# Key norms of a hybrid RWKV-7 and FoX block: the sum of squares by products with a block of ones, the root on the channels

## The chip, the cores and the metric

The kernel runs on one core of one Trainium2 chip. A core has a matrix engine (TensorE, PE in the profile, with its weight loads as PEld), a vector engine (VectorE, DVE), a scalar engine with lookup tables for functions (ScalarE, ACT), GpSimd (POOL) and SyncE (SP), which here only issues loads. The metric is the time of one execution on the device in microseconds (us).

## The reference, cut to what matters

The input has 256 positions of 2048 channels; 16 learned positions are put in front, so the kernel works on L = 272 positions. One layer projects them, runs RWKV-7 time mixing (16 heads of 64 channels) and FoX forgetting attention (16 heads of 64) beside each other, merges the two under gates and ends with a feed-forward network. The change touches two norms over the 64 channels of a head, at each position:

```python
# RWKV-7: the key that removes from the state
kk = heads((k * k_k).astype(F32))
kk = kk / jnp.maximum(jnp.sqrt(jnp.sum(kk * kk, axis=-1, keepdims=True)), 1e-12)
...
# FoX: queries and keys
def _rms(x, g):
    xf = x.astype(F32)
    xf = xf * lax.rsqrt(jnp.mean(xf * xf, axis=-1, keepdims=True) + RMS_EPS)
    return xf.astype(x.dtype) * g
q = _rms(q.reshape(B, L, FOX_HEADS, HEAD_DIM), q_g)
k = _rms(k.reshape(B, L, FOX_HEADS, HEAD_DIM), k_g)
```

The input of the projections is itself normalised (`_rms(h, n1)`). The kernel leaves the factor 1/rms of each position (`rsb`) out of the weight products and brings it in behind them.

## The kernel before, in words

**Weight products.** Every number is float32. For the matrix engine a number is split in a high half, which is its value in the engine's short float32r form, and a low half, the rest; a product is then made of three (high by high, high by low, low by high). Weights come in blocks of 128x1024 (512 KB). `wload` makes one: SyncE issues the load into `raw`, ScalarE copies it to the high half `wh` (L350), VectorE subtracts to get the low half `wl` (L351). Each of `raw`, `wh` and `wl` has three buffers, so `wh` of block n+3 is written when TensorE is done with block n. The products of channels by positions are L361, L362, L363 (272 or 258 columns) and, where only the 256 real positions are wanted, L420 and L422, with high and low half of the activations side by side in 512 columns.

**Groups.** The heads are worked in four groups of four. For each group g the loop runs, on TensorE, the weight products of RWKV's k, v and r (256 columns of weights each), of the small low-rank maps (`sig`, `aa`, `g`), of FoX's q, k and v, and two jobs of output gates (`zg`); behind the four groups come the remaining gates, the branches, the output and the feed-forward network (`gt`, `up`, `dn`).

**Order of the work.** The work that doesn't use weights (norms, state updates, attention) is written as generators, which the code calls streams. A clock of estimated nanoseconds runs with the weight products: after each product group `slot(ns)` adds its estimate, and when a stream's due time has come, its next stage is emitted at this place, one stage at a slot. A stage ends in `yield delay`, which sets the next due time. TensorE's instructions stand in exactly the order in which the code emits them (`manual_schedule`); the other engines' instructions are ordered by a scheduler that models their durations, and each engine then runs them strictly in its order, waiting for the operands of the next one. Of the on-chip sums (PSUM), four banks hold weight products and four (`aux_ps`) are for the streams.

**RWKV's k norm** (`rwkv_bg`, one stream per group). ScalarE makes `kk` = k times `k_k` and its square `sq`. In `head_sums` six float32 products have a tile of squares (positions as rows) as weights and `bsum`, two columns of ones for the two heads of a tile, as moving data; the sums lie with positions on the partitions, 12 numbers each. The profile counts each float32 product twice (`ss`, L383). Nine small VectorE passes (`rsqrt_steps`, L239 to L248, in two stages) give the root's reciprocal from the bits of the number and two refinements. `spread` copies it on ScalarE to 64 channels per head; six float32 transposes on TensorE bring it back to channels by positions (`kx`, L387), and VectorE multiplies `k` by it from PSUM (L708). Then come the decay's scans and exponentials, the operands `ar` and `bk` (L735, L732), and the products `mat`. A later stage of the same stream, group by group, is the normalised output `Y` (L960), which TensorE transposes (`yT`, L387), 4200 ns (`NORM`) of the clock later.

**FoX's norms** (`fox_jobs`). The squares of q (`sqf`, two halves) go through `head_sums` (`fss`: four float32 products, eight rows), and so do the squares of k (six products, twelve rows). A stream `norms` waits for both, takes the root of all 20 numbers at once, and spreads k's part back as above (`fx`, six transposes, a multiplication of `kn`). q's root stays with positions on the partitions, where the attention uses it as a scale (`hs`, `hr`). The attention `fox_bg` waits for `ready`, loads its bias and goes on to the scores `sc`.

The state update of group g-1 (`u`, `y`, `s` and copies, in the `step` stages) runs beside the beginning of group g.

## Time and profile before

| | |
|---|---|
| three runs | 1586.58, 1588.59, 1588.29 us |
| median | 1588.29 us |
| the profiled execution | 1585.63 us, of it the span of the page 1583.9 us |
| granted TensorE clock | 1.0 |
| TensorE, products | busy 1573.6 us (99%), 10292 |
| TensorE, weight loads | busy 1371.4 us (87%) |
| VectorE | busy 1007.9 us (64%), 1849 |
| ScalarE | busy 771.5 us (49%), 1133 |
| GpSimd | busy 109.7 us (7%), 207 |

How to read the rows. A row of a timeline gives the start in us from the span's beginning, the length, the engine, the line of the kernel, the operation, output<-input by the program's names, sizes, and how many like instructions in a row it stands for (x); a bracket tells how long the engine had been idle before it and what ended that. Weight products overlap, so the distance of two starts, and not the length, is what a product takes of TensorE's time. A row of groups gives busy time and mean nanoseconds of one, then the idle time just before these instructions with what ended it. A row of stretches gives from:to, then PE with its busy time, the sum of its weight loads and products (with counts), VectorE, ScalarE and GpSimd busy in the stretch, the granted clock, the share of the DMA engines and GB/s.

### The profile page before, as it was taken

The numbers are of one execution on the slowest core, as the hardware profiler recorded it, in microseconds if no ns is written. First come the engines' busy times: TensorE is split into PE (matmuls) and PEld (weight loads), VectorE is DVE, ScalarE is ACT, GpSimd is POOL, SyncE is SP. The second block draws the span as 40 slices with busy tenths as digits, with TensorE's granted clock in tenths as the row PEclk, the third lists the DMA queues.
The fourth block names the chain that finished last, engine by engine and source line by source line (L and its number), as shares of the span: only waits on it lengthen the run. The fifth ranks groups of instructions, "written<-read, shape, count | busy, mean of one in ns | idle before, by whom it ended". The sixth has DMA issues, their size and how long they took to land.

```text
span 1583.9 us, 26384 instructions
## 1 busy us (share of the span) xinstructions
PE 1573.6 (99%) x10292; PEld 1371.4 (87%) x10292; DVE 1007.9 (64%) x1849; ACT 771.5 (49%) x1133; POOL 109.7 (7%) x207
## 2 busy tenths in 40 slices
PE   8999999999999999999999999999999999999998
PEld 7998988889889878999888888888888888888887
DVE  5777677768868856776556656655666566444443
ACT  6555455455445544654445544544455445333332
POOL 4103102203101200000000000000000000000000
PEclk9999999999999999999999999999999999999999
DMA  7655546545544556776756666666666666566664
GB/s 204 177 156 167 146 121 174 167 127 142 167 143 139 169 161 176 243 227 210 225 178 180 184 195 186 186 186 187 186 186 184 189 186 187 188 204 203 188 200 132
DMA packets 217132, 283.34 MB, mean 179 GB/s; under 512 B 26554, under 2 KB 134704, under 8 KB 217008
## 3 DMA queue, kind: packets, MB, share of 16 engines
q1 hardware_dynamic: 212144, 277.68, 59.6%
q10 hardware_dynamic: 4320, 3.93, 0.7%
q8 instruction: 81, 1.33, 0.3%
q14 instruction: 43, 0.35, 0.1%
q0 software_dynamic: 544, 0.05, 0.0%
HBM read 274.43 MB, written 7.19 MB: 178 GB/s over the span
## 4 chain that ended last, share of the span: by engine, by line
PE 99%; DVE 0%; DMA 0%; ACT 0%; SPq 0%; issue 0%; ACTq 0%
PE up L420 10%; PE gt L420 10%; PE zg L420 8%; PE dn L1255 5%; PE dn L1256 5%; PE dn L1254 5%; PE up L422 5%; PE gt L422 5%; PE zg L422 4%; PE f L361 2%; PE f L420 2%; PE f L363 2%; PE f L362 2%; PE br L362 2%; PE br L363 2%; PE br L361 2%
## 5 line engine op out<-in xcount | busy, mean ns | idle before, releaser
L351 DVE TENSOR_TENSOR wl<-raw,wh 128x1024 fp32r<-128x1024 f32 (+2 forms) x512 | 613.5, 1200 | 447.4 <-ACT wh L350 446.4
L350 ACT ACTIVATE wh<-raw 128x1024 fp32r<-128x1024 f32 (+2 forms) x512 | 530.1, 1038 | 613.3 <-PE dn L1255 142.4
L420 PE MATMUL gt<-hts,wh 128*128 128x512 f32 x704 | 247.0, 398 | 0.0
L420 PE MATMUL up<-hts,wh 128*128 128x512 f32 x704 | 247.0, 398 | 0.0
L422 PE MATMUL gt<-hts,wl 128*128 128x256 f32 x660 | 185.5, 281 | 0.0
L422 PE MATMUL up<-hts,wl 128*128 128x256 f32 x660 | 185.2, 281 | 0.0
L420 PE MATMUL zg<-xhl,wh 128*128 128x512 f32 x512 | 184.6, 404 | 0.0
L420 PEld LDWEIGHTS up<-hts,wh 128*128 128x128 f32 x704 | 130.1, 188 | 28.8
L420 PEld LDWEIGHTS gt<-hts,wh 128*128 128x128 f32 x704 | 129.9, 188 | 28.6
L1255 PE MATMUL dn<-wh,acl 128*128 128x512 f32 x352 | 138.9, 395 | 0.0
L1256 PE MATMUL dn<-wl,ach 128*128 128x512 f32 x352 | 138.9, 395 | 0.0
L1254 PE MATMUL dn<-wh,ach 128*128 128x512 f32 x352 | 138.9, 395 | 0.0
L422 PE MATMUL zg<-xhl,wl 128*128 128x256 f32 x480 | 135.0, 281 | 0.0
L422 PEld LDWEIGHTS up<-hts,wl 128*128 128x128 f32 x660 | 124.6, 189 | 1.9
L422 PEld LDWEIGHTS gt<-hts,wl 128*128 128x128 f32 x660 | 124.6, 189 | 1.9
L420 PEld LDWEIGHTS zg<-xhl,wh 128*128 128x128 f32 x512 | 94.4, 188 | 21.6 <-issue 1.8
L422 PEld LDWEIGHTS zg<-xhl,wl 128*128 128x128 f32 x480 | 90.6, 189 | 1.1
L1255 PEld LDWEIGHTS dn<-wh,acl 128*128 128x128 f32 x352 | 66.3, 188 | 15.6
L1254 PEld LDWEIGHTS dn<-wh,ach 128*128 128x128 f32 x352 | 66.3, 188 | 15.5
L1256 PEld LDWEIGHTS dn<-wl,ach 128*128 128x128 f32 x352 | 66.3, 188 | 15.4
L361 PE MATMUL f<-xhl,wh 128*128 128x272 f32 x256 | 77.6, 303 | 0.0
L363 PE MATMUL f<-xhl,wl 128*128 128x272 f32 x256 | 73.8, 288 | 0.0
(467 smaller groups left out, 2798.4 us busy)
## 6 DMA issues: line engine op xcount, KB each, us to landing
raw<-in_w_gate_up_dram SPq DMA_DIRECT2D x176, 512.0 KB, 3.7
raw<-in_w_in_dram SPq DMA_DIRECT2D x160, 512.0 KB, 3.8
raw<-in_w_down_dram SPq DMA_DIRECT2D x88, 512.0 KB, 3.8
raw<-in_w_o_dram SPq DMA_DIRECT2D x32, 512.0 KB, 4.3
raw<-in_w_branch_a_dram SPq DMA_DIRECT2D x16, 512.0 KB, 3.6
raw<-in_w_branch_b_dram SPq DMA_DIRECT2D x16, 512.0 KB, 4.7
zgd<-zg ACTq DMA_DIRECT2D x30, 128.0 KB, 1.8
gate<-zgd SPq DMA_DIRECT2D x15, 256.0 KB, 4.6
```

The lines of the kernel that those rows point to most:

```text
L350: nc.scalar.activation(wh[:prow, cs_], raw[:prow, cs_], AF.Copy)
L351: nc.vector.tensor_tensor(wl[:prow, cs_], raw[:prow, cs_], wh[:prow, cs_].bitcast(F32), op=ALU.subtract)
L361: nc.tensor.matmul(ps, wh, ah, start=first, stop=False)
L362: nc.tensor.matmul(ps, wh, al, start=False, stop=False)
L363: nc.tensor.matmul(ps, wl, ah, start=False, stop=last)
L420: nc.tensor.matmul(ps.rearrange("p (a t) -> p a t", a=2), wh, act, start=first, stop=last)
L422: nc.tensor.matmul(ps[:, :T], wl, act[:, 0, :], start=False, stop=False)
L1254: nc.tensor.matmul(box[t], ah[:, kt, ts_], wh[:, k, :], start=first, stop=False)
L1255: nc.tensor.matmul(box[t], al[:, kt, ts_], wh[:, k, :], start=False, stop=False)
L1256: nc.tensor.matmul(box[t], ah[:, kt, ts_], wl[:, k, :], start=False, stop=last)
```

## The change

Three things are done in another way.

First, for RWKV's k and FoX's k the sum over a head and its way back to the channels become one step. The squares (channels by positions, 128x272 for each half m of the group) are split in float32r high and low halves (`nh` on ScalarE, `nl` on VectorE), and each half is multiplied with `bones`, the 128x128 matrix with two blocks of 64x64 ones, which the kernel already has for another sum. The result has, on each channel, its head's sum. Per norm these are four float32r products of 272 columns, where there were 6 float32 products with 2 columns (12 rows) and 6 transposes.

Second, the root is taken on all channels: a floor or an added term comes out of PSUM on VectorE into the place of the squares (`floor`), ScalarE takes Ln and then Exp with scale -0.5, which is a first value of the root's reciprocal, and five VectorE passes over 128x272 per half (ten in all, L634 to L638 of the changed kernel) refine it and multiply `kk` or `kn`. In between stand two delays of the clock, `N_SUM` = 1200 and `N_ROOT` = 2000; `X_RS`, `X_SPREAD` and `Y_SPREAD` go.

Third, FoX's q keeps its way (`head_sums`, small passes, now over 8 numbers, in `q_norms`, a stream of its own), and k gets `k_norms`. The term added to k's mean square was `eps1`, with positions on the partitions; it is now `epsw`, over channels by positions, made once at the start by three VectorE operations, among them a reciprocal over 128x272. The Ln and Exp of FoX's norm write into a tile that shares its single buffer with the attention's bias. GpSimd's eight memsets for padded sums go.

```diff
+    epsw = xp.tile([P, L], F32, tag="epsw", name="epsw")
...
             nc.vector.tensor_copy(rsb, prb)
+
+            nc.vector.tensor_tensor(epsw, rsb, rsb, op=ALU.mult)
+            nc.vector.reciprocal(epsw, epsw)
+            nc.vector.tensor_scalar(epsw, epsw, RMS_EPS, None, op0=ALU.mult)
...
+    def head_norms(xs, root, dst, floor, name):
+        parts = []
+        for m in range(2):
+            hi, lo_ = (zt_(f"{n}{name}{m}")[:, :L].bitcast(F32R) for n in ("nh", "nl"))
+            split(hi, lo_, xs[m])
+            parts.append((hi, lo_))
+        yield N_SUM
+        pss = []
+        for m in range(2):
+            ps = aux_ps(f"{name}{m}")[:, :L]
+            for i, part in enumerate(parts[m]):
+                clock[2] += L / 2.4
+                nc.tensor.matmul(ps, bones, part, start=i == 0, stop=i == 1)
+            pss.append(ps)
+        for m in range(2):
+            floor(xs[m], pss[m])
+        ys = root()
+        for m in range(2):
+            nc.scalar.activation(ys[m], xs[m], AF.Ln)
+        for m in range(2):
+            nc.scalar.activation(ys[m], ys[m], AF.Exp, scale=-0.5)
+        yield N_ROOT
+        for m in range(2):
+            x_, y_ = xs[m], ys[m]
+            nc.vector.tensor_tensor(x_, x_, y_, op=ALU.mult)
+            nc.vector.tensor_tensor(x_, x_, y_, op=ALU.mult)
+            nc.vector.scalar_tensor_tensor(x_, x_, -10.0 / 3.0, x_, op0=ALU.add, op1=ALU.mult)
+            nc.vector.scalar_tensor_tensor(y_, x_, 5.0, y_, op0=ALU.add, op1=ALU.mult)
+            nc.vector.scalar_tensor_tensor(dst[:, m, :], y_, 0.375, dst[:, m, :], op0=ALU.mult, op1=ALU.mult)
...
-        for d, ps in head_sums(kn_, [sq[:, m, :] for m in range(2)], L, f"ss{g}"):
-            nc.vector.tensor_scalar(d, ps, 1e-24, None, op0=ALU.max)
-        yield from rsqrt_steps(rw, kr_, kn_, [P, 12], "kt")
-        backs = [spread(kr_, m, L, f"kx{g}{m}") for m in range(2)]
-        yield Y_SPREAD
-        for m in range(2):
-            nc.vector.tensor_tensor(kk[:, m, :], kk[:, m, :], backs[m](), op=ALU.mult)
+        def root():
+            y = et(f"ny{g}")
+            return [y[:, m, :] for m in range(2)]
+        yield from head_norms([sq[:, m, :] for m in range(2)], root, kk,
+                              lambda x_, ps: nc.vector.tensor_scalar(x_, ps, 1e-24, None, op0=ALU.max), f"ss{g}")
         yield Y_KK
...
+        def q_norms(sqs):
+            for i, (d, ps) in enumerate(head_sums(hs, sqs, f"fss{g}")):
+                nc.vector.tensor_scalar(d, ps, 1.0 / HD, eps1[:, i:i + 1], op0=ALU.mult, op1=ALU.add)
+            yield from rsqrt_steps(fx, hr, hs, [P, 8], "ht")
+
+            nc.vector.tensor_tensor(hs, hs, hr, op=ALU.mult)
+            ready.append(1)
+
+        def k_norms(sqs):
+            def root():
+                y = fx.tile([P, 2, L], F32, tag="bias", name=f"fy{g}", bufs=1)
+                return [y[:, m, :] for m in range(2)]
+            yield from head_norms(sqs, root, kn,
+                                  lambda x_, ps: nc.vector.scalar_tensor_tensor(
+                                      x_, ps, 1.0 / HD, epsw, op0=ALU.mult, op1=ALU.add), f"fk{g}")
             ready.append(1)
...
-                    spawn(sums(sqs, dst, n), SUMS)
-                    if dst is kn:
-                        spawn(norms(), PREP)
+                    spawn((q_norms if dst is qn else k_norms)(sqs), SUMS)
...
-        while not ready or not gate_done:
+        while len(ready) < 2 or not gate_done:
```

The scheduler orders the engines anew. The rows below are instructions in an engine's order: line, operation, output<-inputs, size and count. A name is the program's name with its group's digit and a number of its tile.

VectorE at RWKV's k norm of group 1, before: the floors (L703) and small passes of the root between low halves of weights (`wl`) and copies of the state (`sv`).

```order
L351 TENSOR_TENSOR wl_2798<-raw_2796,wh_2797 128x1024
L703 TENSOR_SCALAR kn1_2778<-ss1_2780 128x4 x2
L703 TENSOR_SCALAR kn1_2778<-ss1_2780 16x4
L239 TENSOR_SCALAR kr1_2779<-kn1_2778 128x12
L240 TENSOR_TENSOR kt_2791<-kr1_2779 128x12
L241 SCALAR_TENSOR_TENSOR kt_2791<-kn1_2778,kt_2791 128x12
L351 TENSOR_TENSOR wl_2844<-raw_2842,wh_2843 128x1024
L242 SCALAR_TENSOR_TENSOR kr1_2779<-kt_2791,kr1_2779 128x12
L244 TENSOR_TENSOR kt_2791<-kr1_2779 128x12
```

The same place after the change: floors (L718), ten passes with nothing between them, FoX's q halves (L431), and only then the next `wl`.

```order
L718 TENSOR_SCALAR sq1_2774<-ss10_2841 128x272
L718 TENSOR_SCALAR sq1_2774<-ss11_2844 128x272
L634 TENSOR_TENSOR sq1_2774<-sq1_2774,ny1_2849 128x272 x2
L635 TENSOR_TENSOR sq1_2774<-sq1_2774,ny1_2849 128x272 x2
L636 SCALAR_TENSOR_TENSOR sq1_2774<-sq1_2774 128x272 x2
L637 SCALAR_TENSOR_TENSOR ny1_2849<-sq1_2774,ny1_2849 128x272 x2
L638 SCALAR_TENSOR_TENSOR k1_2000<-ny1_2849,k1_2000 128x272 x2
L431 TENSOR_TENSOR qn1_2676<-qn1_2676,f01_0_2732 128x256
L431 TENSOR_TENSOR qn1_2676<-qn1_2676,f01_1_2733 128x256
L355 TENSOR_TENSOR wl_2909<-raw_2907,wh_2908 128x1024
```

The floor's result goes to ScalarE and comes back as `ny1` between the second and the third of these rows, so VectorE stands there until Exp is done.

VectorE around the scaled output `Y` in group 1, before: `Y` (L960), then FoX's root passes, the meta products' masks (L767), and one `wl` before the copies out of `yT` (L973).

```order
L960 TENSOR_TENSOR Y0_2506<-Y0_2506,s20_3063 128x512
L241 SCALAR_TENSOR_TENSOR ht_3209<-hs1_2647,ht_3209 128x20
L242 SCALAR_TENSOR_TENSOR hr1_2648<-ht_3209,hr1_2648 128x20
L244 TENSOR_TENSOR ht_3209<-hr1_2648 128x20
L245 SCALAR_TENSOR_TENSOR ht_3209<-hs1_2647,ht_3209 128x20
L246 SCALAR_TENSOR_TENSOR ht_3209<-ht_3209 128x20
L247 TENSOR_SCALAR ht_3209<-ht_3209 128x20
L767 TENSOR_TENSOR NK01_3095<-mat010_3223,mup_77 80x2x16
L767 TENSOR_TENSOR NK01_3095<-mat011_3224,mup_77 80x2x16
L248 TENSOR_TENSOR hr1_2648<-ht_3209,hr1_2648 128x20
L351 TENSOR_TENSOR wl_3303<-raw_3301,wh_3302 128x1024
L973 COPY ya_118<-yT0_3255 64x4x64 x2
```

After: FoX's low half of the squares (L492), the masks (L777) and a `wl` stand ahead of `Y` (L970).

```order
L492 TENSOR_TENSOR nlfk11_3176<-sqf11_3142,nhfk11_3175 128x272
L244 TENSOR_TENSOR gt_3065<-s20_3042 128x8
L777 TENSOR_TENSOR NK01_3074<-mat010_3194,mup_77 80x2x16
L245 SCALAR_TENSOR_TENSOR gt_3065<-s10_3041,gt_3065 128x8
L777 TENSOR_TENSOR NK01_3074<-mat011_3195,mup_77 80x2x16
L246 SCALAR_TENSOR_TENSOR gt_3065<-gt_3065 128x8
L355 TENSOR_TENSOR wl_3282<-raw_3280,wh_3281 128x1024
L247 TENSOR_SCALAR gt_3065<-gt_3065 128x8
L248 TENSOR_TENSOR s20_3042<-gt_3065,s20_3042 128x8
L970 TENSOR_TENSOR Y0_2459<-Y0_2459,s20_3042 128x512
L983 COPY ya_119<-yT0_3226 64x4x64 x2
```

On TensorE `yT` itself moves up: it stood in the third of the four blocks of FoX's v weights and now stands in the second, three products behind the last of `mat`; the block whose `wh` buffer `wh_3281` takes over is the first.

ScalarE at RWKV's k norm of group 0, after: between the two high halves of the squares (L491) stands a `wh` of weights, and the two table loads stand before Ln and before Exp.

```order
L712 ACTIVATE sq0_1174<-k0_591 128x544
L491 ACTIVATE nhss00_1191<-sq0_1174 128x272
L354 ACTIVATE wh_1235<-raw_1234 128x1024
L491 ACTIVATE nhss01_1195<-sq0_1174 128x272
L628 ACT_TABLE_LOAD
L628 ACTIVATE ny0_1221<-sq0_1174 128x272 x2
L630 ACT_TABLE_LOAD
L630 ACTIVATE ny0_1221<-ny0_1221 128x272 x2
L430 ACTIVATE qn0_1085<-f00_0_1141 128x256
```

Before, `sq0` was followed there by weight blocks and the copies of `spread`; there was no table load in the norm.

More of the change, by code (lines that the diff above doesn't have):

```diff
@@ L592, in forget_gate, with head_sums @@
         gate_done.append(1)
[L596 to L599 removed]
+    def head_sums(dst, sqs, name):
         ps = aux_ps(name)
[L603 to L605 removed]
+        for i in range(2):
             for m in range(2):
                 c = 4 * i + 2 * m
[L608 to L609 removed]
@@ L611, in spread @@
[L611 to L624 removed]
+                pe_mm(ps[:, c:c + 2], sqs[m][:, i * P:(i + 1) * P], bsum, start=True, stop=True)
@@ L1021, in f @@
                         continue
-                    sq = fx.tile([P, L], F32, tag="sqf", name=f"sqf{g}", bufs=3)
+                    sq = sqf(m)
                     if dst is qn:
```

55 lines of the change are left out of this document (8 added, 47 removed).

## The prediction

> **What bounds the kernel now.** I read the page first, then the mean load by stretch, then TensorE's timeline product by product.
>
> ```profile
> PE 1573.6 (99%) x10292; PEld 1371.4 (87%) x10292; DVE 1007.9 (64%) x1849; ACT 771.5 (49%) x1133; POOL 109.7 (7%) x207
> ...
> PE 99%; DVE 0%; DMA 0%; ACT 0%; SPq 0%; issue 0%; ACTq 0%
> ```
>
> The chain of waits is TensorE's own row from end to end, so a product taken out of its row is time gained, and one put in is time lost, as long as TensorE never waits. What feeds it is near its limit in the stretch that the change touches: the table by stretches gives, for 200 to 250 us (PE, PEld, DVE, ACT, POOL busy),
>
> ```profile
> 200.00:250.00 50.00, 50.00 (x457) 45.16 (x456) 40.68 (x101) 27.69 (x45) 4.86 (x9) 1.00 0.47 131
> ```
>
> VectorE works 81% of it. Each block of weights needs a high half on ScalarE (`wh`) and then a low half on VectorE (`wl`), and `wh` has three buffers:
>
> ```profile
> L350 ACT ACTIVATE wh<-raw 128x1024 fp32r<-128x1024 f32 x488 | 516.9, 1059 | 602.7 <-PE dn L1255 142.4 <-PE up L420 125.3 <-PE gt L420 110.1
> ```
>
> ScalarE's idle time before `wh` ends with a product: block n+3 can be split only when TensorE is through with block n.
>
> **What the products cost and save.** TensorE's timeline in group 0, at the float32 sums of k and at the transposes:
>
> ```profile
> 86.17 0.28 PE L422 MATMUL f<-xhl,wl 128*128 128x256 f32 x1
> 86.29 1.14 PE L383 MATMUL ss<-bsum,sq 128*128 128x2 f32 x12
> 87.36 0.50 PE L420 MATMUL f<-xhl,wh 128*128 128x512 f32 x1
> 87.70 0.28 PE L422 MATMUL f<-xhl,wl 128*128 128x256 f32 x1
> ...
> 93.83 0.29 PE L361 MATMUL f<-xhl,wh 128*128 128x272 f32 x1
> ...
> 94.08 0.29 PE L363 MATMUL f<-xhl,wl 128*128 128x272 f32 x1
> 94.20 1.08 PE L387 MATMUL kx<-ident,kx 128*128 128x128 f32 x6
> 95.21 0.39 PE L361 MATMUL f<-xhl,wh 128*128 128x272 f32 x1
> 95.44 0.29 PE L362 MATMUL f<-xhl,wh 128*128 128x272 f32 x1
> ...
> 110.67 1.13 PE L383 MATMUL fss<-bsum,sqf 128*128 128x2 f32 x12
> ...
> 120.47 0.28 PE L801 MATMUL bs<-rkh,bones 128*128 128x256 f32 x1
> ...
> 120.95 0.29 PE L361 MATMUL f<-xhl,wh 128*128 128x272 f32 x1
> ...
> 124.39 1.07 PE L387 MATMUL fx<-ident,fx 128*128 128x128 f32 x6
> ```
>
> Durations overlap, so a block is priced by starts. Between two weight products of the same kind two pairs apart lie 0.35 us (86.17 to 87.70 without the sums); the sums make it 1.53, so they cost 1.18. Two steps of 272 columns take 0.25 (93.83 to 94.08); the transposes make 1.36 of it, 1.11. FoX's k sums and transposes are the same instructions (12 and 6). Removed per group: 2 x 1.18 + 2 x 1.11 = 4.58; of four groups **18.3**. Added: 2 x 4 float32r products with `bones` of 272 columns at 0.125 (the four of 256 columns at 120.47 took 0.48, with no step after them): 1.0 a group, **4.0**. If TensorE never waited, the change would be worth **-14.3 us**.
>
> **What the other engines get.** For each of eight norms ScalarE loses two spreading copies and gets two splits, two Ln, two Exp and two table loads; VectorE loses small root passes and two multiplications and gets two low halves, two floors and ten passes over 128x272. These are hidden only while `wl` and the small results come in time. Rows of group 1 that price them, and TensorE's marks there:
>
> ```profile
> 203.91 1.28 ACT L667 ACT_TABLE_LOAD   x1 [0.89 <-PE sig L363]
> 205.20 0.87 ACT L667 ACTIVATE sig<-sig,vcol 128x272 f32<-128x272 f32 x2
> ...
> 211.21 0.66 ACT L698 ACTIVATE sq<-k 128x544 f32<-128x544 f32 x1
> ```
>
> ```profile
> 223.70 0.78 DVE L708 TENSOR_TENSOR k<-k,kx 128x272 f32<-128x272 f32 x2
> ...
> 228.81 1.21 DVE L351 TENSOR_TENSOR wl<-raw,wh 128x1024 fp32r<-128x1024 f32 x1
> 229.94 0.68 DVE L735 TENSOR_TENSOR ar<-r,dd 128x512 f32<-128x512 f32 x1
> ...
> 233.48 0.68 DVE L732 TENSOR_TENSOR bk<-kf,cs 128x512 f32<-128x512 f32 x1
> ...
> 242.47 0.16 DVE L242 SCALAR_TENSOR_TENSOR s<-gt,s 128x8 f32<-128x8 f32 x1
> 242.55 0.20 DVE L995 TENSOR_SCALAR hs<-fss,eps 16x4 f32<-16x4 f32 x1
> ...
> 246.32 0.69 DVE L960 TENSOR_TENSOR Y<-Y,s 128x512 f32<-128x512 f32 x1
> ```
>
> ```profile
> 204.79 0.40 PE L420 MATMUL f<-xhl,wh 128*128 128x512 f32 x1
> ...
> 205.37 0.28 PE L422 MATMUL f<-xhl,wl 128*128 128x256 f32 x1
> 205.57 0.45 PE L383 MATMUL u<-R,X 64*64 64x64 f32 x8
> ...
> 206.53 0.28 PE L422 MATMUL f<-xhl,wl 128*128 128x256 f32 x1
> ...
> 225.31 0.84 PE L383 MATMUL fss<-bsum,sqf 128*128 128x2 f32 x7
> ...
> 236.69 0.71 PE L383 MATMUL mat<-ar,bk 64*128 64x128 f32 x8
> ...
> 248.07 0.60 PE L387 MATMUL yT<-ident,Y 128*128 128x128 f32 x4
> ```
>
> From starts: a 128x272 pass on VectorE 0.35 when the next doesn't need it, 0.43 alone; 512 columns 0.60; `wl` 1.13; an interleaved small pass 0.1; ScalarE 0.44 a 128x272, a table load 1.29 to the next instruction. Before, everything was early: `bk` was written at 234.16 for a product at 236.69, Y at 247.0 for 248.07.
>
> **Groups 1 to 3.** Time is counted from the group's first q product (204.79). Undisturbed, TensorE would reach three marks much sooner than before:
> - yT, before at 43.3: less 1.62 (a u block is 1.16 - 0.35 = 0.81, 205.37 to 206.53; it and an s block alike now stand ahead of the q products), 0.68 (ss 1.18 to 0.50), 1.11 (kx), 1.17 (fss of k), 3.02 (it stands in the second block of v weights, no longer the third: 24 x 0.126). **35.7.**
> - mat, before at 31.9: without the 1.17, and likewise a block earlier: **25.5.**
> - fss of q, before at 20.5: less 1.62, 0.68, 1.11 and 0.38 (three products), plus 0.81 (u and y of the last step now ahead): **17.5.**
>
> Now VectorE's row. The `bones` products come at about 9.5 and wait for nothing (the low halves are done at 7.3). The floors stand behind a `wl` and the state update and end at 11.3. Ln follows the first floor: 11.0 to 11.8; the Exp load to 13.1; the two Exp to 13.6 and 14.0. VectorE can take nothing out of turn and idles 2.3 us. Ten passes at 0.35: 17.2; the two q halves: 17.9. ScalarE squares the second at 18.45, and fss, whose second product was due at 17.75, **waits 0.8**. VectorE goes on without a gap: `wl` 1.13, state copies 0.55, scans 1.4, small 0.2, 0.63, `wl` 1.13 (23.05), then seven passes of 256 to 544 columns with q's small root passes between them, 4.7, to the last write of `bk` at 27.8. mat is due at 25.5 + 0.8 = 26.2 with its second product's slack: **waits 1.7**, and the weights behind it 0.1. From 27.8 to the scaled Y: five `wl` (5.7), `rkl`, two reductions, four masks, the mean's subtraction (eight at 0.6: 4.8), two low halves 0.7, some 20 small 2.2, Y 0.65: 41.8. yT is due at 35.7 + 2.6 = 38.3: **waits 3.5**. Behind it the FoX k norm does the same with two ya copies ahead of its Ln load (Exp at 48.5, passes to 53.3, `wl` 54.5 for a gate block due at 54.05): **0.45**. Sum 6.6 a group, three groups: **19.8**.
>
> One part of this needs no walk. Y's scaling now stands behind a `wl` whose `wh` reuses the buffer that TensorE frees 1.46 us before it reaches yT; `wh` 1.06, `wl` 1.13, two small 0.3, Y 0.69, and the 0.4 from the last product's start to its release, make 3.5: yT waits at least 2.1.
>
> **Group 0** has no state passes. The square ends at 86.14 (before: 85.48 + 0.66). Between the two splits stands a `wh`:
>
> ```profile
> 86.37 1.06 ACT L350 ACTIVATE wh<-raw 128x1024 fp32r<-128x1024 f32 x1 [0.22 <-PE f L420]
> ```
>
> so the second high half ends at 88.0, the second low half, behind its `wl`, at 89.2; its product is due at 86.29 + 1.40 (eight products later than ss) + 0.38 = 88.07: **waits 1.2**. The same reckoning gives fss **1.1** and mat **2.0**. FoX's k norm has over 1 us in hand here. **4.3.**
>
> **The start.** `epsw` is made where VectorE had split the first k block:
>
> ```profile
> 38.98 1.22 DVE L351 TENSOR_TENSOR wl<-raw,wh 128x1024 fp32r<-128x1024 f32 x1
> ```
>
> ```profile
> 44.63 0.29 PE L363 MATMUL k<-xhl,wl 128*128 128x272 f32 x1
> ```
>
> ```profile
> L1095 DVE RECIPROCAL sums<-sums 128x4 f32<-128x4 f32 x8 | 1.4, 174 | 3.2 <-ACT s L1090 3.2
> ...
> L703 DVE TENSOR_SCALAR kn<-ss 128x4 f32<-128x4 f32 x8 | 0.9, 157 | 4.9 <-PE ss L383 4.9
> ```
>
> That `wl` now stands behind the lerps of the two LoRA rows and the low half of tanh (ready at 43.3), so it starts at 44.8, ends at 46.0 and k's third product **waits 1.4**. The reciprocal over 272 columns isn't in the trace. If its columns cost what a pass's do it is 0.43; if all of the 17 ns that it takes longer over four columns is per column, 1.6, and the wait 1.9. I take 1.4, since tanh hides about 1 us of it.
>
> At nothing I cost POOL's eight memsets less, and FoX's bias load, which now stands behind fewer weight loads on SP but can go only when Exp's tile is free: 17 us remain to the scores.
>
> **The sum:** -14.3 + 19.8 + 4.3 + 1.4 = **+11.2**. The profiled execution took 1585.63 (span 1583.9), so 1596.8; the runs' median, 1588.29, is 2.7 higher: 1599.5, say **1599**.
>
> The Trainium skill, ScalarE: Activation LUTs, "What ACT_TABLE_LOAD costs", puts a switch of sets at about 2.66 us, load and drain. Here the next ACTIVATE starts 1.29 after the load does (203.91, 205.20), so the row decides; by the page the Exp switch alone would add 1.38 to VectorE's row in each k norm, some 5 to 10 us in all. The same page holds that Ln and Exp share a set and need one load ("natural_log_exp_and_others has both"); in the built order a load stands before each, and by the page the sum would be about 5 us smaller.
>
> **The rivals.**
> - *The products alone* (1574): every wait above is absorbed, as all were before. For it: margins of 4 us and more on most `wl`. Against it: the waits at yT and in group 0 follow from the rows' order alone. 8%.
> - *Only the waits that the order forces*: 3 x 2.1, 1.0 in group 0, 1.4 at the start, because VectorE takes its passes faster than I let it, or ScalarE starts earlier. -14.3 + 8.7 = -5.6: 1583, and up to 1591 with half of the rest. 20%, half of it within 0.2%.
> - *A dearer switch*, the side of much slower: the Ln load doesn't run ahead but waits with its operand, as in the row at 203.91, whose load stood 0.89 for a product. 1.28 more on VectorE's row in each RWKV norm and at the gate block behind each FoX norm of groups 1 to 3, 1.28 x 7 = 9: 1608. It decides as soon as VectorE is the later one, as it is from 13.6 on. 15%.
> - *Forecast*, 1592 to 1606: 57%.
>
> A measurement of this kernel tells 0.2%, 3.2 us, from no change. Faster: 8 + 9 = 17%; same 11%; slower 72%. Range: 1586 (half of the second rival outside) to 1609 (past the third).
>
> **What would show it.** Right: the sums and transposes gone (18 us), eight blocks of `bones` products of about 0.5; TensorE idle or its products stretched before fss, mat and yT in groups 1 to 3, yT most, released by VectorE or ScalarE; VectorE idle about 2 us before the first of the ten passes, released by Exp; 12 more table loads. Wrong: TensorE's row as dense as before between 85 and 600 us, or yT without a wait; also if the ten passes take under 0.3 us each, or if the first k block doesn't wait.

## The result, and the profile after

The changed kernel takes 1609.67 us (median of four runs, 1609.16 to 1610.28) where the kernel before takes 1587.63: a ratio of 1.0139, 95% interval 1.0122 to 1.0157, 22 us slower. The forecast was 1599 with a range to 1609: the sign is right, the size is half of what came. The profiled execution took 1609.78 us, span 1607.8, which is 23.9 more than before.

The page of the changed kernel, its first row and the shares of its chain of waits:

```profile
PE 1573.8 (98%) x10180; PEld 1370.7 (85%) x10180; DVE 1034.0 (64%) x1888; ACT 793.8 (49%) x1177; POOL 106.6 (7%) x199
...
PE 90%; DVE 7%; ACT 1%; issue 1%; DMA 1%; SPq 0%; DVEq 0%; ACTq 0%
```

The chain is no longer TensorE's row alone; VectorE sets the end for 7% of the span. TensorE has 112 products fewer and is busy as long as before. The view of the waits of TensorE lists what it stood for (total us, how often, the longest). In the kernel before it has only entries of the first microseconds (`xT`, `pn`, `prb`); now, behind those:

```profile
PE yT L391 <- DVE Y L970: 9.9, 3, 3.3
PE mat L387 <- DVE ht L247: 3.9, 3, 1.3
...
PE zg L426 <- DVE wl L355: 3.4, 2, 2.4
...
PE k L367 <- DVE wl L355: 1.9, 1, 1.9
PE fss L387 <- ACT sqf L1032: 1.8, 4, 0.7
PE mat L387 <- DVE bk L742: 1.3, 1, 1.3
PE ss L622 <- DVE nlss L492: 0.9, 1, 0.9
```

23.1 us of waiting, 19.7 of it at marks that the forecast named; the `zg` row (3.4) stands where it had put nothing. It had priced all waits at 25.5. So the waits are not where the other half comes from. TensorE's timeline in group 1 shows it, around `yT`:

```profile
255.36 0.29 PE L367 MATMUL f<-xhl,wl 128*128 128x272 f32 x1
258.97 0.63 PE L391 MATMUL yT<-ident,Y 128*128 128x128 f32 x4 [3.32 <-DVE Y L970]
...
259.80 0.29 PE L622 MATMUL fk<-nhfk,bones 128*128 128x272 f32 x1
259.93 0.29 PE L622 MATMUL fk<-nlfk,bones 128*128 128x272 f32 x1
...
260.30 0.37 PE L365 MATMUL f<-xhl,wh 128*128 128x272 f32 x1
...
260.92 0.43 PE L365 MATMUL f<-xhl,wh 128*128 128x272 f32 x1
261.15 0.43 PE L366 MATMUL f<-xhl,wh 128*128 128x272 f32 x1
```

Behind the wait the products with `bones` start 0.13 apart, as forecast, and the four of them take 0.50 (259.80 to 260.30); from 260.4 on the weight products start 0.23 apart, half the pace, and have no wait beside them. The table by stretches says why. The borders here are chosen: 3.41 us apart, at the moments where the recorded clock changes and on the grid that they make (columns: from:to, PE busy, weight loads, VectorE, ScalarE, GpSimd, granted clock, DMA share, GB/s):

```profile
45.32:48.73 3.41, 1.54 (x12) 1.32 (x11) 3.35 (x8) 1.38 (x2) 0.00 (x0) 1.00 0.00 0
48.73:52.15 3.42, 3.42 (x18) 3.42 (x17) 3.38 (x6) 1.70 (x2) 0.10 (x1) 0.50 0.80 196
52.15:55.56 3.41, 3.41 (x29) 3.41 (x29) 2.24 (x4) 2.17 (x5) 0.00 (x0) 1.00 0.81 254
137.48:140.89 3.41, 1.48 (x7) 0.80 (x5) 3.17 (x9) 2.94 (x4) 1.30 (x2) 1.00 0.01 2
140.89:144.31 3.42, 2.81 (x9) 2.42 (x10) 3.21 (x10) 0.00 (x0) 0.00 (x0) 0.50 0.48 131
144.31:147.72 3.41, 3.41 (x13) 2.93 (x12) 1.99 (x5) 1.06 (x1) 0.00 (x0) 0.50 0.85 221
...
243.29:246.71 3.42, 2.13 (x24) 1.81 (x24) 3.42 (x11) 0.63 (x1) 0.00 (x0) 1.00 0.11 36
246.71:250.12 3.41, 3.41 (x27) 3.13 (x28) 3.41 (x8) 2.63 (x5) 0.00 (x0) 1.00 0.54 153
...
253.53:256.95 3.42, 2.11 (x21) 1.71 (x19) 3.27 (x13) 1.06 (x1) 0.57 (x1) 1.00 0.90 216
256.95:260.36 3.41, 1.39 (x12) 1.42 (x13) 2.12 (x5) 0.38 (x1) 2.02 (x4) 1.00 0.62 168
260.36:263.77 3.41, 3.41 (x17) 3.41 (x17) 2.10 (x6) 2.79 (x5) 0.00 (x0) 0.50 0.72 167
```

Read the PE column against the clock of the next row. Where TensorE was busy 1.54, 1.48 or 1.39 of 3.41 us, the next stretch ran at 0.50; where it was busy 2.13 or 2.11 (the wait before `mat` at 245, the first part of the wait before `yT`), the next ran at 1.00. Six stretches of this kernel are at 0.50 (one behind the start's wait, two behind the gate block of group 0, one behind `yT` in each of groups 1 to 3): 6 x 3.41 x 0.5 = 10.2 us of clock. TensorE was busy in 19.4 of these 20.5 us, so that about 9.7 us were lost, and no term of the forecast held them.

So the account, start to start on TensorE: -14.3 by the products (the forecast's figure), +27.2 by waits and the refilling behind them, +9.7 by the clock, together 22.6 of 23.9. About 0.6 of that is counted twice, since `yT` of group 3 and the gate block of group 0 start inside a slow stretch. And 1.35 us are not the change's: at 36 us, ahead of all that it touches, the same products already stand 1.35 later than before, about 0.9 by a load of the first positions that came late at 10 us, the rest because the first full clock came at 14.60 us here and at 12.28 before. Set side by side, the same products stand 10.7 us later than before when group 1 begins, 14.1, 17.9 and 21.7 one, two and three groups on, and 23.8 to 23.9 from 627 us to the end: the whole loss lies in the stretch that the change touches.

### The profile page after: what moved, and what is told of

Its sections match the earlier page's. It is cut to its first block, busy times and chain, and to the rows that moved or that the text cites. A ratio compares the mean times of both kernels' runs of the same rounds, so it can differ in the third digit from the quotient of the medians.

```text
span 1607.8 us, 26216 instructions
## 1 busy us (share of the span) xinstructions
PE 1573.8 (98%) x10180; PEld 1370.7 (85%) x10180; DVE 1034.0 (64%) x1888; ACT 793.8 (49%) x1177; POOL 106.6 (7%) x199
## 4 chain that ended last, share of the span: by engine, by line
PE 90%; DVE 7%; ACT 1%; issue 1%; DMA 1%; SPq 0%; DVEq 0%; ACTq 0%
PE up L424 10%; PE gt L424 10%; PE zg L424 8%; PE dn L1260 5%; PE dn L1261 5%; PE dn L1259 5%; PE up L426 5%; PE gt L426 5%; PE zg L426 4%; DVE wl L355 2%; PE br L367 2%; PE br L365 2%; PE br L366 2%; PE wo L1260 2%; PE wo L1259 2%; PE wo L1261 2%
## 5 line engine op out<-in xcount | busy, mean ns | idle before, releaser
L365 PE MATMUL f<-xhl,wh 128*128 128x272 f32 x256 | 78.6, 307 | 0.0
```

What stands on the lines that cost most here:

```text
L365: nc.tensor.matmul(ps, wh, ah, start=first, stop=False)
```

## The experiments

Theory A, formed from this profile: a long wait of TensorE costs its length, and then some microseconds at half clock as well. (That fixed stretches of 3.4 us decide it came with the second run of waits below.) Theory B, its rival: the slow products are late operands, and a wait costs its length. The other question is what makes the waits: the burst of VectorE passes, the table loads before it, or the places at which the stages stand. Each run's time is given against the kernel before on the same chip.

### Waits of known length in the kernel before

```diff
+    def probe():
+        seen[0] += 1
+        if seen[0] % 5 or not steps:
+            return
+        n = steps.pop(0)
+        ps = aux_ps("hopa")[:, :P]
+        nc.tensor.transpose(ps, ident, ident)
+        nc.scalar.activation(hop[0], ps, AF.Copy)
+        for i in range(n):
+            nc.gpsimd.tensor_copy(hop[(i + 1) % 2], hop[i % 2])
+        nc.tensor.transpose(aux_ps("hopb")[:, :P], hop[n % 2], ident)
```

(called ahead of each block of the down products, whose TensorE row was fixed for it; the second run has `nc.scalar.activation(..., AF.Copy)` for the GpSimd copy)

> The kernel before, without the change, with seventeen artificial waits in its last part (the down products, far from what was changed): a transposition on TensorE, a copy on ScalarE, 0 to 8 copies of 128x128 on GpSimd, one after the other, and a transposition that waits for the last. One every five weight blocks, about 13 us apart; the waits should be from about 0.7 to 5 us. Theory A: the shortest waits leave the granted clock at 1.0; from some length near 2 us on a stretch of 3 to 6 us at a clock of 0.5 follows, so that the loss is the wait plus about 2 to 3 us; the yT-like waits of 1.6 us at the mat products, which left the clock alone, and the 2.2 us one at the start, which didn't, put the edge between them. Theory B (no clock effect of its own): the loss equals the wait for all lengths. The Trainium skill, TensorE: Matmul & The Clock Gate, holds that the clock halves after an idle window of some 3.4 us; by that only the probes of 3 us and more would do it.

> The kernel before with twenty artificial waits in the down products, as in the first run of that kind, but made of 1 to 5 more copies on ScalarE instead of GpSimd, four of each, every four weight blocks, for waits between about 1 and 3.5 us. In the first such run a wait of 2.85 and one of 3.2 us halved the clock and others of 2.84, 3.21 and 3.56 did not; all of 3.9 and more did. Theory A (the clock is judged over fixed stretches of time, so that the place of the wait in them decides): between about 2.2 and 3.6 us some waits do it and some of the same length don't, below 2 us none, and a slow stretch lasts 3 to 6 us. Theory B (a fixed length decides, and the first run's mixture is an accident of its shortest products): one edge, the same for all.

One execution each: 1667.53 and 1641.75 us. Over both runs, the distance of the two transpositions' starts and how many of that length were followed by products at half pace:

```
1.2 to 1.9 us     0 of 10
2.3 to 2.6 us     3 of 10
2.8 to 3.0 us     2 of 6
3.2 to 3.6 us     2 of 4
3.9 to 5.0 us     7 of 7
```

The mixture that theory A of the second run expected is there, and no length between 2.3 and 3.6 us decides. What decides is the place. Two waits of the second run, both 2.3 us long by that distance and 2.0 us idle, by the table of stretches, the first three rows for one, the others for the other, each on the grid of 3.41 us that this execution's clock changes make:

```profile
1370.46:1373.87 3.41, 1.47 (x7) 1.25 (x8) 1.23 (x1) 1.79 (x5) 0.00 (x0) 1.00 0.59 162
1373.87:1377.28 3.41, 3.41 (x10) 2.63 (x9) 0.00 (x0) 0.87 (x1) 0.00 (x0) 0.50 0.42 145
1377.28:1380.70 3.42, 3.42 (x16) 2.77 (x16) 1.22 (x1) 1.22 (x2) 0.00 (x0) 1.00 0.18 44
1510.41:1513.82 3.41, 2.01 (x10) 1.34 (x8) 1.85 (x2) 1.65 (x4) 0.00 (x0) 1.00 0.65 201
1513.82:1517.23 3.41, 2.82 (x13) 2.34 (x14) 0.60 (x1) 0.51 (x2) 0.00 (x0) 1.00 0.64 211
```

The first wait lies within one stretch, which is left with 1.47 us of work: the next runs at 0.50. The second is cut by a border into 1.40 and 0.60 of idle time: nothing happens. In all fourteen traces (the kernel before, the changed one and the twelve runs here) the clock changes only on such a grid; of the stretches at full clock in which TensorE had idle time, 37 were followed by a slow one, 34 of these with 1.83 us or more of idle time (the others 1.35, 1.35 and 1.63), and none with more than 1.90 was followed by a fast one. A slow stretch lasted one time or two. A little over half an idle stretch is enough, then, and so a wait of 2.3 us can do it, and those of 3.9 and more all did. Theory B is out: the slow products run where the recorded clock is 0.50, and past the first microseconds the two traces list no wait over 0.2 us but those that were put in. The size fits as well: these waits and 1.7 us for each slow stretch make 78.6 of the 81.9 us, and 46.7 of the 56.1, by which the two spans lie above that of the kernel before (the transpositions themselves are in the rest).

The Trainium skill, TensorE: Matmul & The Clock Gate, section Part 1 (the HAM clock gate), has the stretch right ("4096 cycles @ 1.2 GHz = 3413 ns", free-running), but asks for a whole idle stretch before the clock halves. The first row of the last table had 1.94 us of idle time and was followed by half the clock, and the measurement decides.

### Work put into the waits

```diff
+    def fill(ps, n):
+        for _ in range(n):
+            nc.tensor.matmul(ps, bones, xh[:, 0, :], start=True, stop=True)
...
         ps = aux_ps(f"yT{g}")
+        if g < 3:
+            fill(ps[:, :L], 24)
```

(and 14 in the first k block, 18 ahead of the gate block)

> The changed kernel with more work: products that nobody needs (bones by 272 columns, into a spare bank) are put on TensorE into its longest waits: 14 ahead of the first k block's third product, 18 ahead of the third gate block of group 0, 24 ahead of yT in groups 0 to 2 (those read 1 to 3 in the trace by their place). Each product takes 0.125 us, so each row of them is a little shorter than the wait it fills, and the product behind it still starts when VectorE is done. Theory A (idle TensorE loses its clock): the granted clock stays near 1.0 behind these places and about 9 us of slow running go, although TensorE has 104 products more: about 1600 to 1602, 1.008 to 1.009. Theory B (products behind a wait are slow because their operands come late): nothing gained, 1609 to 1612, 1.014 to 1.015.

1604.74, ratio 1.0112 (1.0097 to 1.0127): 104 products more, 13 us of TensorE's time, and 5 us faster than the changed kernel; the mean granted clock is 1.000 in all four executions, where it was 0.993 or 0.994. That is theory A's mechanism, at less than the gain that it put on it (1600 to 1602). What took a part of the rest is in the view of the waits:

```profile
PE zg L433 <- DVE wl L356: 3.9, 5, 1.0
...
PE k L374 <- DVE wl L356: 0.8, 1, 0.8
```

The gate blocks of groups 1 to 3, which had no wait in the changed kernel, now wait 0.9 each: TensorE is earlier by what the clock gave and meets the next late `wl`.

### Stages moved one by one

```diff
-NORM = 4200
+NORM = 8400
```

> The changed kernel with one number changed: the scaled Y's delay before yT on TensorE is 8400 instead of 4200, so that yT stands about 5 us further on in TensorE's row of each group. In the changed kernel's profile yT waits 3.4 to 3.9 us in groups 1 to 3, and behind each wait the products run at a granted clock near 0.5 for about 3 us. Theory A (a wait of this length also halves the clock for some us, and that is a cost of its own): the three waits go, 10.5 us, and the slow stretches with them, about 4.5 us more: 1609.7 - 15 = 1595, 1.0045 of the kernel before. Theory B (only the waits cost, the slow rows are another effect that stays): 1599, 1.007. Theory C (VectorE is simply too late, and the next product that needs it waits instead): 1605 or more, 1.011.

1612.68, 1.0170 (1.0153 to 1.0187), 3 us above the changed kernel, with intervals that just overlap. The wait before `yT` is gone, and the view has instead

```profile
PE zg L426 <- DVE wl L355: 13.8, 5, 4.0
...
PE trbk L391 <- ACT bt L825: 2.9, 3, 1.7
```

Theory C of its expectation: VectorE and ScalarE are behind, and whatever stands next waits. The place in the grid shows in the four executions of this one kernel: 1610.41, 1612.34, 1613.02 and 1616.43 us, at mean clocks of 0.997, 0.996, 0.994 and 0.992. FoX's tables were also loaded four times in a row here, Ln and Exp for each half.

```diff
-            nc.vector.tensor_tensor(epsw, rsb, rsb, op=ALU.mult)
-            nc.vector.reciprocal(epsw, epsw)
-            nc.vector.tensor_scalar(epsw, epsw, RMS_EPS, None, op0=ALU.mult)
...
+        nc.vector.tensor_tensor(epsw, rsb, rsb, op=ALU.mult)
+        nc.vector.reciprocal(epsw, epsw)
+        nc.vector.tensor_scalar(epsw, epsw, RMS_EPS, None, op0=ALU.mult)
         gate_done.append(1)
```

> The changed kernel with epsw (its product, reciprocal and scaling on VectorE) made about 40 us later, where the forget gate's columns are copied, and nothing else. In the changed kernel the first k block's third product waits 2.0 us at 46 us, and products run at half pace until 52 us, 2.4 us lost. Theory A (wait and slow clock): 4.4 us gained, 1605.3, 1.0111. Theory B (the wait alone): 1607.6, 1.0126. Theory C (the three operations delay something else as much where they now stand): no gain, 1.0139.

1605.94, 1.0121 (1.0106 to 1.0136): 3.7 us gained, nearer to theory A's 4.4 than to 2.1, though the times alone do not part the two (the interval overlaps that of the changed kernel). The trace does: the start's wait falls from 1.9 to 0.4 and the slow stretch behind it is gone.

```diff
-                    spawn(fox_bg(g, qn, kn, vv, hs, hr, ready), HOP)
+                    spawn(fox_bg(g, qn, kn, vv, hs, hr, ready), 6000)
```

> The changed kernel with the first attention stage (the transpositions pv of v and their copies vt) 6000 behind v instead of 3050, and nothing else. In the changed kernel's profile the third gate block of group 0 waits 2.7 us: ScalarE has vt in its row ahead of that block's high half and stands until pv is done; with the later stage the high half stands ahead of vt. Theory A: this wait goes with the slow stretch behind it, 2.7 + 3.0 = 5.5 us less, 1604, 1.010, nothing changes in the other groups. Theory B (the block's load is what is late, since VectorE freed its buffer late): the wait stays within 1 us of what it was: 1608 to 1610, 1.013.

1613.02, 1.0164 (1.0149 to 1.0179). In group 0 theory A holds: the gate block's wait goes. But TensorE, some 4 us earlier, stands at `fss` in groups 1 and 3, where a `wl` now lies between the floors and Ln:

```profile
PE fss L387 <- ACT sqf L1032: 5.3, 3, 2.3
```

Nine stretches run at half clock instead of six. "Nothing changes in the other groups" was wrong, and the whole did not gain.

### One part, and the load of VectorE

RWKV's norm alone, with FoX's as before (the diff of the change without `q_norms`, `k_norms` and `epsw`):

> RWKV's k norm alone in the new way; FoX's norms, epsw and its wait as in the kernel before. Saved on TensorE: 4 x (1.18 + 1.11 - 0.5) = 7.2 us. Theory A (each norm's burst delays what stands next on VectorE): ss of group 0, fss and mat wait about as in the changed kernel, 3.7 in group 0 and 2.0 in each of the others, and yT, which has no split squares of FoX ahead of it, 1 to 2 us each without a slow clock: 7.2 less than 13 to 16, so 1594 to 1596, 1.004 to 1.0055. Theory B (FoX's part makes nearly all of the loss): faster than before, 1583, 0.997. Theory C (RWKV's part makes it): 1602 or more, 1.009.

1598.52, 1.0074 (1.0059 to 1.0089), between theories A and C. `yT` waits 2.0 us a time with nothing of FoX's new work ahead of it, against 3.3 with the whole change.

```diff
-            nc.vector.tensor_tensor(x_, x_, y_, op=ALU.mult)
-            nc.vector.tensor_tensor(x_, x_, y_, op=ALU.mult)
-            nc.vector.scalar_tensor_tensor(x_, x_, -10.0 / 3.0, x_, op0=ALU.add, op1=ALU.mult)
-            nc.vector.scalar_tensor_tensor(y_, x_, 5.0, y_, op0=ALU.add, op1=ALU.mult)
-            nc.vector.scalar_tensor_tensor(dst[:, m, :], y_, 0.375, dst[:, m, :], op0=ALU.mult, op1=ALU.mult)
+            nc.vector.tensor_tensor(dst[:, m, :], y_, dst[:, m, :], op=ALU.mult)
```

> The changed kernel without the refinement of the root: behind Ln and Exp only one VectorE pass per half is left, which multiplies the key by Exp's result; the eight passes that refine it are left out, so the root has the precision of the tables. Theory A (the burst of ten passes on VectorE is what makes fss, mat and yT late): VectorE's row is 8 x 0.35 = 2.8 us shorter at each norm, which is more than fss (0.64) and mat (1.36) wait and most of yT's 3.4 to 3.9; those waits and the slow clock behind yT go: 3 x 2 + 9 + 4.5 = 19.5 less, 1590, 1.002, unless the gate blocks wait in their place as they did when only yT was moved (3.4 us in each of three groups): then 1600, 1.008. Theory B (the table loads and the idle time in front of the passes do it, not the passes): under 6 us gained, 1604 or more, 1.0105.

1595.04, 1.0051 (1.0036 to 1.0066): 14.6 us less, between theory A's two figures. `mat` waits no more, `yT` 4.1 in all, the gate blocks 7.2, and three stretches are slow.

```diff
-            nc.scalar.activation(ys[m], xs[m], AF.Ln)
+            nc.scalar.activation(ys[m], xs[m], AF.Copy)
...
-            nc.scalar.activation(ys[m], ys[m], AF.Exp, scale=-0.5)
+            nc.scalar.activation(ys[m], ys[m], AF.Copy, scale=0.0)
```

> The changed kernel with Ln and Exp replaced by plain copies (the second with scale 0), so that the sixteen switches of tables in the norms go, while the ten passes stay; the norms' results are then zero. In the changed kernel VectorE stands 2.2 us before the first pass of each RWKV norm, most of it the two loads (1.28 each). Theory A (all time on VectorE's row between the floor and the last pass counts, idle or busy): up to 2.6 us less per norm, nearly what the eight refining passes take (2.8), so nearly the same gain as leaving these out (14.6): 1595 to 1600, 1.005 to 1.008. Theory B (the passes alone make the waits, the idle time falls where VectorE has nothing else to do): under 5 us gained, 1605 or more, 1.0105.

1599.53, 1.0082 (1.0065 to 1.0099): 10.1 us less, at theory A's upper end. The waits sum to 20.5, hardly less than 23.1, but in the profiled execution no stretch is slow. That is place and not length: the longest wait, 2.5 us before `mat` of group 0, is cut by a border of the grid into 1.24 and 1.28. The other executions took 1597.63, 1600.18 and 1602.19 at clocks of 1.000, 0.998 and 0.996, so that the gain holds some luck. Of the 10.1 us only 2.6 are waiting; most is the clock.

```diff
         for m in range(2):
             nc.vector.tensor_tensor(kk[:, m, :], kk[:, m, :], backs[m](), op=ALU.mult)
+        for _ in range(4):
+            for m in range(2):
+                nc.vector.tensor_tensor(kk[:, m, :], kk[:, m, :], unit, op=ALU.mult)
```

(in the kernel before, and the same for `kn`; `unit` is a tile of ones)

> The kernel before, with its old norms, and eight more VectorE passes over 128x272 behind each of the eight k norms: the normalised key is multiplied by ones, four times for each half, 2.8 us each time. TensorE's products are those of the kernel before. Theory A (VectorE's burst alone makes TensorE wait): bk was 2.4 us and Y 1.1 us ahead of TensorE in the kernel before, so mat waits about 0.4 and yT or a gate block 1.5 to 3 in each group, some with a slow clock: 8 to 15 us slower, 1595 to 1602, 1.005 to 1.0095. Theory B (the burst is harmless, and the waits of the change come from the new places of its stages): under 3 us, 1.002 or less.

1595.05, 1.0047 (1.0032 to 1.0062): 7.9 us slower with the same products in the same places. The time is theory A's lower edge, the mechanism only a part of it: eight passes, 2.8 us, put behind each norm make `mat` wait, 5.3 us in all with one slow stretch, but `yT` and the gate blocks, which it expected to wait, do not wait at all. So the burst alone does not make the long waits of the changed kernel; its order of stages or its table loads have a part in them (without the loads, above, `yT` waits 1.2 a time, without the refinement 1.4).

```profile
PE mat L385 <- DVE bk L737: 2.8, 3, 0.9
...
PE mat L385 <- DVE bk L738: 2.5, 1, 2.5
```

### All stages later, with and without the refinement

```diff
-NORM = 4200
+NORM = 6500
-N_SUM = 1200
-N_ROOT = 2000
+N_SUM = 2400
+N_ROOT = 4000
-Y_AB = 4400
+Y_AB = 5600
```

(`epsw` late, FoX's q sums at 2800, `fox_bg` at 5000; the second run also without the refinement)

> The changed kernel, all its arithmetic kept, with the stages that use the norms put later on TensorE: epsw made late as in its own run, N_SUM 2400 (1200), N_ROOT 4000 (2000), Y_AB 5600 (4400), NORM 6500 (4200), FoX's q sums 2800 (2000), and the first attention stage 5000 behind v (3050). Theory A (every wait is a stage that stands too early for VectorE and ScalarE, and the products are really 14.3 us cheaper): most waits go and the clock stays at 1.0; 1575 to 1585, 0.992 to 0.998 of the kernel before. Theory B (VectorE and ScalarE are short of time in the stretch, whatever the order, and the weights' halves come late): the waits move to weight blocks, 1595 to 1605, 1.005 to 1.011.

> The same later stages with the refinement left out as in the run without it (one VectorE pass per half behind Exp). Theory A: 1573 to 1580, 0.991 to 0.995, hardly less than with the refinement, since nothing waits for it any more. Theory B (VectorE's load decides): 1580 to 1590, and 10 us or more below the run that keeps the refinement.

With the refinement 1596.35, 1.0058 (1.0043 to 1.0073); without it 1581.66, 0.9967 (0.9954 to 0.9979), which is 0.3% faster than the kernel before. Theory B's times hold in both: with VectorE's load as it is, later places alone do not win. The refinement is worth 14.7 us here, as it was in the changed order (14.6); with it the waits move to the next stage, mostly, and to weight blocks, without it little is left.

The view of the waits with the refinement:

```profile
PE trbk L387 <- ACT ya L980: 8.5, 3, 2.8
PE f L363 <- DVE wl L351: 3.4, 3, 1.2
```

and without it:

```profile
PE zg L422 <- DVE wl L351: 3.0, 4, 0.8
PE ppt L387 <- DVE s L1099: 0.7, 2, 0.5
```

The account closes over all kernels that have the change whole. Their span less (1583.9 - 14.3 + the waits of the view + 1.7 for each slow stretch; the filled one also +13) leaves between 1.6 and 7.2 us. In it are the first loads with the first full clock (0.2 to 2.0 us by the kernel) and the refilling of TensorE behind each wait (0.1 to 0.25 of start distance, 9 to 21 waits):

```
                     waits   slow    span     left
changed kernel        23.1     6    1607.8     4.9
NORM 8400             26.5     3    1608.4     7.2
epsw late             21.7     4    1602.4     4.3
waits filled          13.2     0    1603.0     7.2
no refinement         14.9     3    1593.5     3.9
no tables             20.5     0    1597.1     7.0
fox_bg 6000           24.1     9    1610.6     1.6
all later             15.0     3    1595.3     5.6
all later, no ref.     4.4     0    1580.0     6.0
```

The last column is even to 6 us, and to 3.3 without the one of nine slow stretches (part of which TensorE waited through), over kernels that lie 30 us apart, so waits and slow stretches explain what sets them apart. The 14.3 enters all rows alike; the smallness of what is left bounds its error to a few microseconds. In the last row 1.75 is the start and at most 2.3 the refilling of nine waits, so that about 2 us have no account there: the products may have saved 12 to 14 rather than 14.3.

## Why the prediction was right and where it failed

Term by term, forecast and measured in the changed kernel (start to start, us):

```
                                   forecast   measured
products                            -14.3      -12 to -14 by the account
start, first k block                 1.4        2.0
group 0: ss / fss / mat              1.2 / 1.1 / 2.0   1.3 / 1.1 / 1.3
group 0: gate block                  0          3.0
groups 1 to 3: fss                   0.8 each   0.7
               mat                   1.8 each   1.4
               yT                    3.5 each   3.5, 3.4, 4.0 (0.5 of it clock)
               gate block            0.45 each  0, 0, 0 (1.2 in a later one)
half clock                           not seen   9.7
```

- **The products** that were added were priced right: 0.13 a `bones` product, 0.50 a block in the rows above. What the removed ones saved is known only by the account.
- **VectorE's walk** was right step by step, in group 1 within half a microsecond (the last pass 17.2 behind the first q product, as forecast; the scaled Y 41.3, forecast 41.8). Its idle time before the first pass was put at 2.3 and each pass at 0.35; VectorE's timeline in group 1:

```profile
228.10 0.78 DVE L718 TENSOR_SCALAR sq<-ss 128x272 f32<-128x272 f32 x2
231.11 0.79 DVE L634 TENSOR_TENSOR sq<-sq,ny 128x272 f32<-128x272 f32 x2 [2.24 <-ACT ny L630]
...
234.64 0.74 DVE L431 TENSOR_TENSOR qn<-qn,f 128x256 f32<-128x256 f32 x2
```

  2.24 of idle time, and 3.53 from the first pass to the q halves for ten passes. `yT`'s wait came out within a tenth in groups 1 and 2, and the part that needed no walk (at least 2.1) held as a bound. In group 1 the agreement has some luck in it: the chain that ended last there goes through a weight load, which the walk did not have.

```profile
250.67 4.72 DMA raw<-in_w_in_dram
255.50 1.06 ACT wh L354
256.59 1.22 DVE wl L355
```

  The load began when VectorE's `wl` of an earlier block, late itself, had freed its buffer; VectorE's own row was through 0.14 us before this `wl` could start, so both ways gave nearly the same time. In groups 2 and 3 it is VectorE's row alone, over the last 8 us.
- **The start** was taken at 1.4 with 1.9 as the far end. It came to 2.0: the reciprocal over 272 columns took 1.84 us and the far end (1.9) was the right one.

```profile
41.16 1.84 DVE L274 RECIPROCAL epsw<-epsw 128x272 f32<-128x272 f32 x1
...
46.74 1.21 DVE L355 TENSOR_TENSOR wl<-raw,wh 128x1024 fp32r<-128x1024 f32 x1
```

- **The step that failed** is the sum itself, "-14.3 + 19.8 + 4.3 + 1.4": it prices each wait at its length and has no term for the clock. Two kinds of waits in it (the start, `yT`) and one that it lacks (the gate block of group 0) left TensorE idle for over half of a 3.4 us stretch, and each halved the clock for one or two stretches behind it, 9.7 us. The profile of the kernel before had shown the price once, in TensorE's timeline at its start, where TensorE comes out of a wait:

```profile
10.95 0.43 PE L362 MATMUL lo<-xhl,wh 128*96 128x272 f32 x1
11.18 0.43 PE L363 MATMUL lo<-xhl,wl 128*96 128x272 f32 x1
...
12.39 0.29 PE L362 MATMUL lo<-xhl,wh 128*112 128x272 f32 x1
12.52 0.29 PE L363 MATMUL lo<-xhl,wl 128*112 128x272 f32 x1
```

  The same two products start 0.23 apart there, and 0.13 apart from 12.4 us on. The page's clock says 1.00 for both, because its record begins with the first change, at 12.28.
- **The gate block of group 0** is the second miss, 3.0 us. It was put at nothing ("over 1 us in hand"): what the forecast says of group 0 follows VectorE's norm and not ScalarE's row behind it. ScalarE's timeline:

```profile
136.74 0.84 ACT L1058 ACTIVATE vt<-pv,rsk 128x256 f32<-128x256 f32 x2 [3.38 <-PE pv L391]
137.47 2.95 ACT L354 ACTIVATE wh<-raw 128x1024 fp32r<-128x1024 f32 x3
```

  It stood 3.4 us for `pv`, with three high halves behind `vt` in its row. With the stage of `pv` and `vt` later (`fox_bg` at 6000) the wait went, so this cause is shown; why the scheduler set them so is not.
- **The rivals.** "A dearer switch" gave 1608, nearly the time that came, by a mechanism that did not happen: that it came near is luck. In RWKV's norms the Ln load ran ahead of its operand (below, 0.61 us idle behind it) and VectorE idled what the forecast had said; the gate blocks behind FoX's norms of groups 1 to 3 do not wait. "Only the waits that the order forces" and "the products alone" are out; the version without refinement and with later stages ends 8 us above the second.

```profile
226.67 1.28 ACT L628 ACT_TABLE_LOAD   x1
228.56 0.78 ACT L628 ACTIVATE ny<-sq 128x272 f32<-128x272 f32 x2 [0.61 <-DVE sq L718]
```

What stays open is how much of `yT`'s wait is the ten passes, how much the idle time before them and how much its new place, and the part of the 14.6 us of the refinement that is VectorE's time itself and the part that the scheduler makes of it by a new order; each kernel's order is another.

## What to carry to other kernels

Price a wait of the bounding engine by its length and by its place: of the waits put in (their length by the distance of starts), those of up to 1.9 us cost themselves alone, from 2.3 on some also cost a stretch or two at half clock, and from 3.9 on all did. So a few short waits can be cheaper than one long one, and products that nobody needs can pay for themselves. Work taken from TensorE and given to VectorE can be worth nothing where VectorE feeds TensorE: eight passes behind each norm, 2.8 us, cost 7.9 us in the kernel before and 14.6 in the changed one, where the whole change saves 14.3 at most on TensorE. When a single wait is removed, look for the next mark on the same feeder before counting it as gained.

## What the runs showed of the hardware that was not expected

The clock is judged on a fixed grid of 3.413 us: in each of the fourteen traces all changes fall on it. A stretch at full clock in which TensorE idled over 1.9 us was always followed by a slow one, one with under 1.3 never. Of 49 slow stretches twelve were followed by another, ten of these with 0.6 to 2.3 us of idle time; the 37 that ended had 0.63 or less. So two stayed slow without idle time, and two of the drops came with 1.35; that lighter products count for less than weight products would fit, and was not tested. The reciprocal on VectorE took 1.84 us for 272 columns, four times the 0.44 of the two-operand pass ahead of it. Ln and Exp, in turn, each loaded a table, 1.28 us a time, and where the order alternated them by halves (`NORM` at 8400) there were four loads for one norm.
